# A conv branch's output projection by a seven-product scheme, its outer sums done by accumulating DMAs

## The chip, the cores and the metric

The kernel runs on one core of one Trainium2 chip. The metric is the device time of one execution in microseconds (us). Before the change it is 2522.57 us, the median of three runs (2522.21 to 2522.71).

## The reference

One inference step of a small encoder trunk with two layers. 640 frames (512 of a new stream, 8 x 16 of running streams) of 1024 channels go through, per layer, half a feed-forward step, a mixer, and another half feed-forward step. The change is in the mixer:

```python
z = h @ w_in                       # conv B | conv C | conv V | q | k | v | gates
g = sigmoid(g + b_gate); g_conv, g_attn = split(g)
y_conv = B * causal_conv3(C * V)   # 512 channels
y_attn = band_attention(q, k, v)   # 8 heads of 64
m = g_conv * (y_conv @ w_conv_out) + g_attn * (y_attn @ w_attn_out)
x = x + m @ w_o
```

`w_conv_out` and `w_attn_out` are 512 x 1024, `w_o` is 1024 x 1024, all in fp32.

## The kernel before

Activations lie transposed: channels on the 128 partitions, the 640 frames (T) along the free dimension, in two halves t1 and t2 of 320 columns (HT). A matmul multiplies a 128 x 128 weight tile with 128 x 320 columns. For precision every fp32 operand is split into a high part in fp32r (`hi`, a cast on ScalarE) and a rest (`lo`, a subtraction on VectorE), and a product is three matmuls: hi x hi, lo x hi, hi x lo.

Weights come from one stream in HBM (`wst`), 128 x 1024 at a time, loaded by SyncE's queue (SP) into three buffers `raw`. ScalarE casts each to `whi`, VectorE subtracts to `wlo`; both have three buffers. One such 1024-wide (or 512-wide) weight part is called a slab. `slab()` hands out the next slab and prepares those after it, `flush()` issues VectorE's subtractions that are pending, `quiet()` takes a slab that is ready, `prep` begins one more, `ahead` and `begin` begin the one after.

Many projections are done by a scheme of seven products instead of eight (Strassen's, in Winograd's form), where pairs of row tiles and the two halves of the frames form the 2 x 2 blocks. `gate_pair(m)` (L1263) is one such mixing of two output tiles, m and m + 1, of the gates: seven blocks of twelve matmuls, in the order X11, X21, N6, T5, T7, X22, T4, into three banks pa, pb, pc; four slabs, three of them with sums of weight tiles made on VectorE (four additions of 512 columns). Banks that go on accumulating must be copied out in between: c1 after the first block, u2 after the third, c5 after the fourth (ScalarE); VectorE adds these copies to what comes later, multiplies with rr (the norm's factor), and ScalarE makes the sigmoids.

`outputs` (L1253) is the mixer's last part but for w_o. Its order before: gate pair 2, four products `out(0)` to `out(3)` of w_conv_out, then three times a gate pair and two products (w_conv_out's 4 to 7 behind pairs 4 and 6), then pairs 8 to 14, each with two products of w_attn_out. `product` (L387, matmuls at L374) multiplies all four row tiles of the 512 inputs: 24 matmuls of 320 columns into one two-bank tile py, which VectorE multiplies with the gate. `take`, called in pair 2, splits the four tiles of y_conv. The matmuls of `block` are at L397, the casts of weights at L307, their subtractions at L312, additions at L251.

In this part PE, VectorE and ScalarE run in the order in which the code issues the instructions (`tc.manual_schedule(engines=ORDERED)`); each engine's queue is in order.

`down_rows` (L936) does the feed-forward's second projection by the same scheme and already sends part of its sums by accumulating DMAs from GpSimd's queue (L976).

Of the kernel before, what the change touches and what calls it, by code (L numbers as in the profile page):

```python
# [22 lines left out]
T = SEQ + NB * TS  # L23
HT = T // 2
# [6 lines left out]
KT = D // P  # L31
FT = FF // P
FH = FT // 2
CT = CW // P
# [6 lines left out]
NP = KT // 2  # L41
# [16 lines left out]
XT4, XN6, XT7, X21, X22, X11, XT5 = range(7)  # L58
# [64 lines left out]


def kinds():


    out, inside = [], [False]

    def put(kind):  # L130
        out.append((kind, inside[0]))

    def plain(n):
        for kind in [8] * (n // 8) + [n % 8] * (n % 8 > 0):
# [24 lines left out]
    for l in range(L):  # L159
        ffn(f"a{l}")  # L160
        held = 0
        for what, _ in mixer_order():
            if what == "mix":
# [12 lines left out]


def halves(t):
    return t.rearrange("p (a b) -> p a b", a=2)
# [3 lines left out]
def trunk(ctx: ExitStack, tc: tile.TileContext, xin, wst, small, pbias, samplebias, kcache, vcache,  # L183
# [33 lines left out]
    def tmp(name):  # L217
        return tp.tile([P, UW], F32, tag="t", name=name)[:, :T]
# [31 lines left out]
    def add(out, a, b):  # L250
        DVE.tensor_tensor(out=out, in0=a, in1=b, op=ALU.add)  # L251
# [58 lines left out]
    def flush():  # L310
        for lo, src, hi in pending:
            DVE.tensor_tensor(out=lo, in0=src, in1=hi.bitcast(F32), op=ALU.subtract)  # L312
        pending.clear()
# [73 lines left out]
    def product(ps, ops, at=()):  # L387
        for _ in steps(ps, ops, at):
            pass

    def block(ps, s, half, ops, ks, start, stop):

        for kp in ks:
            w = [z[:, (half * NP + kp) * P : (half * NP + kp + 1) * P] for z in s]
            xh, xl = ops(kp)
            for j, (a, b) in enumerate(((w[0], xh), (w[0], xl), (w[1], xh))):
                PE.matmul(ps, a, b, start=start and kp == 0 and j == 0,  # L397
                          stop=stop and kp == NP - 1 and j == 2, skip_group_check=True)
# [701 lines left out]
    def mixer(l, after):  # L1100
        with tc.tile_pool(name=f"yp{l}", bufs=1, reuse_waits="tile") as yp, \
# [2 lines left out]

            h, st, stats = norm(yp, f"m{l}", O_GM + l * KT, yas[:, 0, :])
            rr = st.rr
            ycp = [yp.tile([P, 2, T], F32, name=f"yc{l}_{c}") for c in range(CT // 2)]
            ycs = [z[:, i] for z in ycp for i in range(2)]
# [78 lines left out]
            with tc.tile_pool(name=f"gp{l}", bufs=1, reuse_waits="tile") as gp, \  # L1187
                 tc.manual_schedule(engines=ORDERED):
                hold[0] = True
                mo = outputs(l, gp, ops.X, st, cs, ycs, yas, sigmoid, gates)  # L1190
        ex = after()
        with tc.manual_schedule(engines=ORDERED):
            hold[0] = True
# [56 lines left out]
        def t5(self, kp):  # L1250
            self.parts(*(z[:, HT:] for z in self.h[2 * kp]), self.a[kp][:, 1])

    def outputs(l, gp, X, st, cs, ycs, yas, sigmoid, gates):  # L1253


        rr, t1, t2 = st.rr, slice(0, HT), slice(HT, T)
        spare = [gp.tile([P, 2, T], F32, name=f"mm{l}_{i}") for i in range(2)]
        mm = ycs + [spare[i // 2][:, i % 2] for i in range(CT)]
        X11, X21, X22, XN6, XT5, XT7, XT4 = (X[i] for i in ("11", "21", "22", "N6", "T5", "T7", "T4"))
        c1, u2, c5 = cs  # L1260
        every = range(NP)

        def gate_pair(m, then=None):  # L1263
            n = f"{l}_{m}"
            pa, pb, pc = (att(f"q{i}{n}")[:, :HT] for i in "abc")
            u, g = gates[m], gates[m + 1] = tmp(f"g{n}"), tmp(f"g{n}_1")
            s0 = quiet()
            block(pa, s0, 0, X11, every, True, True)
            ACT.copy(c1, pa)
            prep(used[0] + 1)  # L1270
            flush()
            if then:
                then()
            block(pb, s0, 1, X21, every, True, True)
            add(u[:, t1], pb, c1)
            s1 = slab(True)[0]
            flush()
            block(pa, s1, 0, XN6, every, False, True)
            ACT.copy(u2, pa)
            block(pc, s1, 1, XT5, every, True, True)  # L1280
            ACT.copy(c5, pc)
            s2 = slab(True)[0]
            block(pa, s2, 0, XT7, every, False, True)
# [4 lines left out]
            block(pc, s2, 1, X22, every, False, True)  # L1288
            add(u[:, t2], pc, u2)
            s3 = slab(True)[0]  # L1290
            DVE.tensor_tensor(out=u, in0=u, in1=rr, op=ALU.mult)
            sigmoid(u, m)
            block(pa, s3, 0, XT4, every, False, True)
            DVE.tensor_tensor(out=g[:, t1], in0=pa, in1=rr[:, t1], op=ALU.mult)
            sigmoid(g, m + 1, -1.0)
            flush()

        def parts(pool, tag, name, src):
# [4 lines left out]
        def out(m, y, then=None):  # L1303

            py = acc(f"py{l}_{m}")
            product(py, y)
            if then:
                then()
            g = gates[m]
            if m < KT:  # L1310
                DVE.tensor_tensor(out=halves(mm[m]), in0=two(py), in1=halves(g), op=ALU.mult)
            else:
                DVE.tensor_tensor(out=halves(g), in0=two(py), in1=halves(g), op=ALU.mult)
                add(mm[m - KT], mm[m - KT], g)
            flush()

        yc, ya, mo = [], [], []

        def take(y, name, srcs):
            for c, src in enumerate(srcs):  # L1320
                y.append(parts(gp, f"y{c}", f"{name}{l}_{c}", src))

        def give(ms):
            for m in ms:
                mo.append(parts(hp, "h", f"m{l}_{m}", mm[m]))

        gate_pair(2, lambda: take(yc, "yc", ycs))
        for m in range(4):
            out(m, yc)
        for m in range(4, 2 * KT, 2):  # L1330
            gate_pair(m, (lambda: take(ya, "ya", [yas[:, c, :] for c in range(CT)])) if m == KT else None)
            y = yc if m < KT else ya
            last = m == 2 * KT - 2
            out(m, y, (lambda: give(range(3))) if last else None)
            out(m + 1, y, (lambda: give(range(3, 6))) if last else None)
        give(range(6, KT))
        return mo

    def attention(l, h, norms, stats, ops, mp, yas, ycp, both, others):
# [421 lines left out]
def _stream(i):  # L1761
# [9 lines left out]
    for l in range(L):  # L1771
# [34 lines left out]
        for what, m in mixer_order():  # L1806
            if what == "v":
                out.append(v.reshape(KT // 2, 2, P, AW).transpose(0, 2, 1, 3).reshape(-1, P, CH))
            elif what == "mix":
                out.append(chunks(held))  # L1810
                held = []

                out.append(chunks([rows[name][a][o::2] for name, a in m for o in range(2)]))
            else:
                held.append(rows[what][m])
        out.append(chunks(held))
# [69 lines left out]
```

## Time and profile before

| | |
|---|---|
| median of 3 runs | 2522.57 us |
| profiled execution | 2522.74 us, span 2521.0 us, granted clock 0.999 |
| TensorE busy | 2502.0 us (99%), 17192 matmuls |
| VectorE busy | 2117.7 us (84%) |
| ScalarE busy | 1325.1 us (53%) |
| GpSimd busy | 185.6 us (7%) |
| DMA | 265.40 MB, mean 105 GB/s |

The profile is of one execution, taken by the hardware profiler. Engines are PE (TensorE matmuls), PEld (its weight loads), DVE (VectorE), ACT (ScalarE), POOL (GpSimd) and SP (SyncE, which issues loads). A row of a timeline gives the start in us, the length, the engine, the line of the kernel, the operation, and the tiles as out<-in; in square brackets stands the idle time just before it and what ended it. A row of groups gives, after the bar, the busy time of the group and the mean of one in ns, and then the idle time before its instructions.

### The profile page before, as it was taken

How to read it: one execution, taken by the hardware profiler on the slowest of the kernel's cores; microseconds unless marked ns; L12 is line 12 of the kernel's file. 1: busy time of each engine (PE TensorE's matmuls, PEld its weight loads, DVE VectorE, ACT ScalarE, POOL GpSimd, SP SyncE). 2: the span in 40 equal slices, each digit the busy share in tenths (PEclk: the TensorE clock that was granted, in tenths of full speed). 3: DMA queues.
4: the chain of work that ended last, by engine and by line, in shares of the span. 5: the costliest groups of instructions: out<-in, count | busy, mean ns of one | idle time of the engine just before them, and what ended most of it. 6: DMA issues, size and time to landing. Idle time of an engine off the chain costs nothing.

```text
span 2521.0 us, 42929 instructions
## 1 busy us (share of the span) xinstructions
PE 2502.0 (99%) x17192; PEld 2441.3 (97%) x17192; DVE 2117.7 (84%) x3347; ACT 1325.1 (53%) x2084; POOL 185.6 (7%) x249
## 2 busy tenths in 40 slices
PE   9999999999999999999999999999999999999998
PEld 9999999888999999999999999998889999999998
DVE  7889888878677899988699999888786768899997
ACT  7445556664444545555455555557644455455553
POOL 0000112111000001000001000021110000010000
PEclk9999999999999999999999999999999999999999
DMA  4233444334222234343224343443342222243434
GB/s 144 76 105 103 115 115 126 107 114 162 76 85 92 75 101 115 105 110 100 84 76 112 110 116 100 115 118 124 129 138 84 76 93 76 86 114 109 123 100 99
DMA packets 99320, 265.40 MB, mean 105 GB/s; under 512 B 9680, under 2 KB 45136, under 8 KB 99120
## 3 DMA queue, kind: packets, MB, share of 16 engines
q1 hardware_dynamic: 69408, 220.76, 26.7%
q0 software_dynamic: 28992, 41.26, 9.3%
q8 instruction: 135, 2.21, 0.4%
q10 hardware_dynamic: 720, 0.65, 0.1%
q14 instruction: 65, 0.53, 0.1%
HBM read 222.70 MB, written 7.94 MB: 91 GB/s over the span
## 4 chain that ended last, share of the span: by engine, by line
PE 92%; ACT 4%; DVE 3%; issue 1%; DMA 0%; DVEq 0%; ACTq 0%
PE pab L397 12%; PE paa L397 11%; PE pcb L397 6%; PE pca L397 6%; PE daa L952 5%; PE py L374 4%; PE po L374 4%; PE qa L397 4%; PE pdb L374 4%; PE dab L952 4%; PE pbb L397 3%; PE pba L397 3%; PE poa L374 2%; PE pda L374 2%; PE pv L1392 2%; PE ma_cv L397 2%
## 5 line engine op out<-in xcount | busy, mean ns | idle before, releaser
L312 DVE TENSOR_TENSOR wlo<-raw,whi 128x1024 fp32r<-128x1024 f32 (+1 forms) x566 | 585.6, 1037 | 177.8 <-ACT whi L307 172.6
L307 ACT CAST whi<-raw 128x1024 fp32r<-128x1024 f32 (+1 forms) x566 | 509.1, 903 | 366.6 <-PE pbb L397 38.6
L307 ACT CAST whi<-s 128x1024 fp32r<-128x1024 f32 (+1 forms) x152 | 144.4, 950 | 279.5 <-issue 89.3
L397 PE MATMUL pab<-xhib,whi 128*128 128x320 f32 x704 | 218.1, 310 | 0.3
L397 PE MATMUL pab<-xhib,wlo 128*128 128x320 f32 x704 | 217.3, 309 | 0.0
L397 PE MATMUL pab<-xlob,whi 128*128 128x320 f32 x704 | 217.2, 309 | 0.0
L397 PE MATMUL paa<-xhia,whi 128*128 128x320 f32 x640 | 198.0, 309 | 1.0 <-ACT c_a L833 0.6
L397 PE MATMUL paa<-xhia,wlo 128*128 128x320 f32 x640 | 197.5, 309 | 0.0
L397 PE MATMUL paa<-xloa,whi 128*128 128x320 f32 x640 | 197.5, 309 | 0.0
L312 DVE TENSOR_TENSOR wlo<-s,whi 128x1024 fp32r<-128x1024 f32 (+1 forms) x152 | 166.3, 1094 | 9.8 <-ACT whi L307 9.8
L397 PEld LDWEIGHTS pab<-xhib,whi 128*128 128x128 f32 x704 | 132.1, 188 | 0.9 <-ACT c_b L833 0.8
L397 PEld LDWEIGHTS pab<-xlob,whi 128*128 128x128 f32 x704 | 132.1, 188 | 0.2
L397 PEld LDWEIGHTS pab<-xhib,wlo 128*128 128x128 f32 x704 | 132.1, 188 | 0.0
L397 PEld LDWEIGHTS paa<-xhia,whi 128*128 128x128 f32 x640 | 120.1, 188 | 1.6 <-ACT c_a L833 0.9
L397 PEld LDWEIGHTS paa<-xloa,whi 128*128 128x128 f32 x640 | 120.1, 188 | 0.1
L397 PEld LDWEIGHTS paa<-xhia,wlo 128*128 128x128 f32 x640 | 120.1, 188 | 0.0
L976 POOL DMA_DIRECT2D x<-c_b x28 | 33.8, 1209 | 1105.6 <-ACT c_b L969 457.8
L397 PE MATMUL pcb<-xhib,wlo 128*128 128x320 f32 x352 | 108.8, 309 | 0.0
L397 PE MATMUL pcb<-xlob,whi 128*128 128x320 f32 x352 | 108.6, 309 | 0.0
L397 PE MATMUL pcb<-xhib,whi 128*128 128x320 f32 x352 | 108.6, 309 | 0.0
L976 POOL DMA_DIRECT2D x<-c_a x36 | 43.6, 1212 | 865.1 <-ACT whi L307 386.4
L251 DVE TENSOR_TENSOR raw<-raw,raw 128x512 f32<-128x512 f32 x152 | 103.7, 683 | 0.8
(681 smaller groups left out, 7943.2 us busy)
## 6 DMA issues: line engine op xcount, KB each, us to landing
raw<-in_wst SPq DMA_DIRECT2D x378, 512.0 KB, 3.5
x<-c_a POOLq DMA_DIRECT2D x36, 320.0 KB, 4.2
x<-c_b POOLq DMA_DIRECT2D x28, 320.0 KB, 4.1
kc<-in_kcache SPq DMA_DIRECT2D x32, 256.0 KB, 3.8
vc<-in_vcache SPq DMA_DIRECT2D x16, 512.0 KB, 4.7
x<-u_a POOLq DMA_DIRECT2D x18, 320.0 KB, 5.4
x<-u_b POOLq DMA_DIRECT2D x14, 320.0 KB, 5.5
bias<-in_pbias POOLq DMA_DIRECT2D x16, 256.0 KB, 3.6
```

The source lines that it names most:

```text
L251: DVE.tensor_tensor(out=out, in0=a, in1=b, op=ALU.add)
L307: ACT.copy(hi[:, d], src[:, c])
L312: DVE.tensor_tensor(out=lo, in0=src, in1=hi.bitcast(F32), op=ALU.subtract)
L374: PE.matmul(ps[:, a, :HT], w, x[:, a * HT : (a + 1) * HT], start=first and j == 0, stop=last and j == 2)
L397: PE.matmul(ps, a, b, start=start and kp == 0 and j == 0, stop=stop and kp == NP - 1 and j == 2, skip_group_check=True)
L952: PE.matmul(ps[u], w, y, start=start and i == 0 and j == 0, stop=i == 1 and j == 2, skip_group_check=True)
L976: POOL.dma_start(rows(r, cols), z, accum_op=ALU.add)
L1392: PE.matmul(pv[t], xx[:, t * P : (t + 1) * P], w[:, kk * AW : (kk + 1) * AW], start=c == 0 and kk == 0 and j == 0, stop=c == KT // 2 - 1 a ...
```

## The change

w_conv_out is no longer computed by eight products but by two calls of a new function `unit`, each for four output tiles: seven blocks of twelve matmuls into two-bank tiles A and B and a pair of banks C. Its operands (`xhi`, `xlo`: X11, X21, X22, T5, T7, T4, N6 for the two pairs of row tiles) are made beforehand in gate pairs 2 and 4 and, for the last `lo` part, in the first unit itself. ScalarE copies the finished sums into the output tile and GpSimd adds the copies made earlier by accumulating DMAs (`put`, `accumulate`). The outputs are kept unweighted and multiplied with the gates later (`weigh`).

The gate pairs 2, 4 and 6 get `direct=False`: VectorE's additions of c1, c5 and u2 are replaced by a ScalarE copy and an accumulating DMA, and the products with rr (`scale`) and the sigmoids (`bend`) are done later, as jobs at named places (`at`, `spot`). In pairs 8 to 14 (`direct=True`) one of three additions is replaced so. The order of the weight stream becomes: gate pairs 2 and 4, unit 0, gate pair 6, unit 4, then pairs 8 to 14 with w_attn_out's products as before.

The core of the diff, cut:

```diff
-    out += gates[:2] + [("co", m) for m in range(4)]
-    for i, g in enumerate(gates[2:]):
-        name, m = ("co", 4 + 2 * i) if i < 2 else ("ao", 2 * i - 4)
-        out += [g, (name, m), (name, m + 1)]
+    out += gates[:3] + [("unit", ("co", 0)), gates[3], ("unit", ("co", 4))]
+    for i, g in enumerate(gates[4:]):
+        out += [g, ("ao", 2 * i), ("ao", 2 * i + 1)]
...
+        def accumulate(out, z):
+            POOL.dma_start(out, z, accum_op=ALU.add)
...
             block(pb, s0, 1, x21, every, True, True)
-            add(u[:, t1], pb, c1)
+            if direct:
+                ACT.copy(u[:, t1], pb)
+                accumulate(u[:, t1], c1)
...
+            if not direct:
+                ACT.copy(u[:, t1], pb)
+                accumulate(u[:, t1], c1)
             block(pa, s2, 0, xT7, every, False, True)
-            add(g[:, t2], pa, c5)
-            DVE.tensor_tensor(out=g[:, t2], in0=g[:, t2], in1=rr[:, t2], op=ALU.mult)
+            if direct:
+                add(g[:, t2], pa, c5)
+            else:
+                ACT.copy(g[:, t2], pa)
+                accumulate(g[:, t2], c5)
...
+        def sum_low(i):
+            return lambda: low(i, slice(0, 4), vs[i])
+        def unit(m0, to):
...
+            s0 = quiet()
+            mul(a, s0, 0, X11, True)
+            copy(z0[:, :, t1], a)
+            prep(used[0] + 1)
+            begin()
+            flush()
+            spot(me, 1)
+            mul(b, s0, 1, X21, True)
+            put(0, t1, b, z0[:, :, t1])
+            s1 = slab(True)[0]
+            flush()
+            mul(a, s1, 0, XN6, False)
+            copy(z0[:, :, t2], a)
+            spot(me, 2)
+            mul(C, s1, 1, XT5, True)
+            copy(z1, C, -1.0)
+            s2 = slab(True)[0]
+            spot(me, 3)
+            mul(a, s2, 0, XT7, False)
+            put(1, t2, a, z1, -1.0)
+            flush()
+            ahead()
+            mul(C, s2, 1, X22, False)
+            put(0, t2, C, z0[:, :, t2])
+            s3 = slab(True)[0]
+            ahead()
+            mul(a, s3, 0, XT4, False)
+            copy(to[:, 1::2, t1], a, -1.0)
+            flush()
+            spot(me, 4)
...
+        at("g2", 1, opening)
+        at("g2", 2, firsts)
+        at("g2", 3, raw_low(0))
+        at("g2", 4, raw_low(1))
+        at("g4", 1, lasts)
+        at("g4", 3, sum_high(0))
+        at("g4", 4, sum_high(1), sum_low(0))
+        at("c0", 1, sum_low(1))
+        at("c0", 2, scale(2))
+        at("c0", 3, bend(2), scale(4))
+        at("c0", 4, bend(4))
+        at("g6", 2, weigh(1, 3))
+        at("g6", 3, weigh(0, 2))
+        at("c4", 2, scale(6))
+        at("c4", 3, bend(6))
+        at("g8", 1, taken(0), taken(1))
+        at("g8", 2, taken(2), weigh(5, 7))
+        at("g8", 3, taken(3))
+        at("g8", 4, weigh(4, 6))
```

`opening` casts X11, X21 and X22 of both pairs on ScalarE (three casts of 640 columns); `firsts` and `lasts` make the sums N6, T5, T7 and T4 on VectorE; `raw_low`, `sum_high` and `sum_low` make the rest of the operands; `taken` splits the four tiles of y_attn.

More of the change, by code (lines that the diff above doesn't have):

```diff
@@ L162, in kinds @@
         for what, _ in mixer_order():
-            if what == "mix":
+            if what in ("mix", "unit"):
                 plain(held)
@@ L1286, in gate_pair @@
+            block(pa, s2, 0, xT7, every, False, True)
+            if direct:
+                add(g[:, t2], pa, c5)
+            else:
+                ACT.copy(g[:, t2], pa)
+                accumulate(g[:, t2], c5)
             flush()
             ahead()
[L1288 to L1293 removed]
+            block(pc, s2, 1, x22, every, False, True)
@@ L1294, in gate_pair @@
+            if direct:
+                add(u[:, t2], pc, u2)
+            else:
+                ACT.copy(u[:, t2], pc)
+                accumulate(u[:, t2], u2)
+            s3 = slab(True)[0]
+            if direct:
+                times(g[:, t2], rr[:, t2])
+                times(u, rr)
+                sigmoid(u, m)
+            block(pa, s3, 0, xT4, every, False, True)
             DVE.tensor_tensor(out=g[:, t1], in0=pa, in1=rr[:, t1], op=ALU.mult)
-            sigmoid(g, m + 1, -1.0)
+            if direct:
+                sigmoid(g, m + 1, -1.0)
@@ L1296, in gate_pair, with scale, job, bend @@
             flush()
+            spot(me, 4)
+        def scale(m):
+            def job():
+                times(gates[m], rr)
+                times(gates[m + 1][:, t2], rr[:, t2])
+            return job
+        def bend(m):
+            def job():
+                sigmoid(gates[m], m)
+                sigmoid(gates[m + 1], m + 1, -1.0)
+            return job
+        v = yc.rearrange("p (i o) (t c) -> p i o t c", o=2, t=2)
+        xhi, xlo = (gp.tile([P, 2, 7, HT], F32R, name=f"x{i}{l}") for i in ("hi", "lo"))
@@ new lines, in outputs, with high, low, opening @@
+        pairs = [{k: (xhi[:, i, c], xlo[:, i, c]) for c, k in enumerate((XT5, XT7, XT4, XN6, X11, X21, X22))}
+                 for i in range(2)]
+        vs = [v[:, i].rearrange("p o t c -> p (o t) c") for i in range(2)]
+        def high(i, c, z):
+            ACT.copy(xhi[:, i, c], z)
+        def low(i, c, z):
+            DVE.tensor_tensor(out=xlo[:, i, c], in0=z, in1=xhi[:, i, c].bitcast(F32), op=ALU.subtract)
+        def opening():
+            high(slice(0, 2), 4, v[:, :, 0, 0])
+            for i in range(2):
+                high(i, slice(5, 7), v[:, i, 1])
@@ new lines, in raw_low, with sum_high, mul, copy @@
+        def raw_low(i):
+            return lambda: low(i, slice(5, 7), v[:, i, 1])
+        def sum_high(i):
+            return lambda: high(i, slice(0, 4), vs[i])
+        def sum_low(i):
+            return lambda: low(i, slice(0, 4), vs[i])
+        def unit(m0, to):
+            n = f"{l}_{m0}"
+            A, B = (acc(f"{i}co{n}") for i in "ab")
+            C = [att(f"c{i}co{n}")[:, :HT] for i in range(2)]
+            a, b = ([z[:, i, :HT] for i in range(2)] for z in (A, B))
+            me = f"c{m0}"
+            def mul(ps, s, half, kind, start):
+                for i in range(2):
+                    for k, pair in enumerate(pairs):
+                        kp = half * NP + 2 * i + k
+                        wh, wl = (z[:, kp * P : (kp + 1) * P] for z in s)
+                        xh, xl = pair[kind]
+                        for j, (w, y) in enumerate(((wh, xh), (wh, xl), (wl, xh))):
+                            PE.matmul(ps[i], w, y, start=start and k == 0 and j == 0,
+                                      stop=k == 1 and j == 2, skip_group_check=True)
+            def copy(out, ps, scale=1.0):
+                for d, z in ((out, two(A if ps is a else B)),) if ps is not C else zip((out[:, 0], out[:, 1]), C):
+                    ACT.activation(d, z, AF.Copy, scale=scale)
+            def put(r, c, ps, z, scale=1.0):
+                copy(to[:, r::2, c], ps, scale)
+                accumulate(to[:, r::2, c], z)
+            s0 = quiet()
[4 more added lines that the diff above has]
+            flush()
+            spot(me, 1)
+            mul(b, s0, 1, X21, True)
[4 more added lines that the diff above has]
+            copy(z0[:, :, t2], a)
+            spot(me, 2)
+            mul(C, s1, 1, XT5, True)
+            copy(z1, C, -1.0)
+            s2 = slab(True)[0]
+            spot(me, 3)
+            mul(a, s2, 0, XT7, False)
[9 more added lines that the diff above has]
+            flush()
+            spot(me, 4)
@@ L1298, in parts, with weigh, job @@
+        def weigh(*ms):
+            def job():
+                for m in ms:
+                    times(mm[m], gates[m])
+            return job
         def parts(pool, tag, name, src):
@@ L1301, in parts, with out @@
             return hi, lo
-        def out(m, y, then=None):
+        ya, mo = [], []
+        def out(m, then=None):
             py = acc(f"py{l}_{m}")
-            product(py, y)
+            product(py, ya)
             if then:
                 then()
[L1309 to L1314, printed above, removed]
+            g = gates[m + KT]
+            DVE.tensor_tensor(out=halves(g), in0=two(py), in1=halves(g), op=ALU.mult)
+            add(mm[m], mm[m], g)
             flush()
[L1317 to L1321, printed above, removed]
         def give(ms):
@@ L1325, in give, with taken, job @@
                 mo.append(parts(hp, "h", f"m{l}_{m}", mm[m]))
[L1327 to L1335, printed above, removed]
+        def taken(c):
+            def job():
+                hi, lo = (z[:, c // 2, :].rearrange("p a b -> p (a b)")[:, (c % 2) * T : (c % 2 + 1) * T]
+                          for z in (xhi, xlo))
+                split(hi, lo, yas[:, c, :])
+                ya.append((hi, lo))
+            return job
+        at("g2", 1, opening)
[17 more added lines that the diff above has]
+        at("g8", 4, weigh(4, 6))
+        gate_pair(2, False)
+        gate_pair(4, False)
+        unit(0, yc)
+        gate_pair(6, False)
+        unit(4, spare)
+        for m in range(0, KT, 2):
+            gate_pair(m + KT, True)
+            last = m == KT - 2
+            out(m, (lambda: give(range(3))) if last else None)
+            out(m + 1, (lambda: give(range(3, 6))) if last else None)
         give(range(6, KT))
+        assert not jobs
         return mo
@@ L1813, in _stream @@
                 out.append(chunks([rows[name][a][o::2] for name, a in m for o in range(2)]))
+            elif what == "unit":
+                out.append(chunks(held))
+                held = []
+                name, a = m
+                out.append(chunks([rows[name][a + r + 2 * u][o::2] for r in range(2) for o in range(2)
+                                   for u in range(2)]))
             else:
```

54 lines of the change are left out of this document (37 added, 17 removed).

## The prediction

> **What bounds the kernel now.** I read the page first (busy times, chain of waits), then the windows of the mixer's output part, where all of the change lies, and then TensorE's, VectorE's and ScalarE's timelines there.
>
> ```profile
> span 2521.0 us, 42929 instructions
> PE 2502.0 (99%) x17192; PEld 2441.3 (97%) x17192; DVE 2117.7 (84%) x3347; ACT 1325.1 (53%) x2084; POOL 185.6 (7%) x249
> ...
> PE 92%; ACT 4%; DVE 3%; issue 1%; DMA 0%; DVEq 0%; ACTq 0%
> ```
>
> TensorE (PE) is the bound: busy for 99% of the span, 92% of the chain. So a matmul that goes is worth its pace, and a wait on TensorE costs its full length; work on other engines costs nothing until TensorE waits for it. The windows of layer 0's output part (gate pair 2, four products, then pairs 4, 6 and 8, each with two products) show how near that is:
>
> ```profile
> 643.80:656.80 13.00, 12.62 (x86) 12.36 (x85) 10.46 (x17) 9.84 (x15) 0.00 (x0) 1.00 0.27 84
> 656.80:670.90 14.10, 14.10 (x98) 14.10 (x97) 8.52 (x12) 3.64 (x5) 0.00 (x0) 1.00 0.22 74
> 670.90:690.30 19.40, 19.40 (x134) 19.40 (x133) 12.54 (x18) 7.54 (x11) 0.00 (x0) 1.00 0.25 82
> 690.30:709.70 19.40, 19.40 (x135) 19.40 (x134) 12.54 (x18) 7.54 (x11) 0.00 (x0) 1.00 0.26 82
> 709.70:729.10 19.40, 19.40 (x134) 19.40 (x134) 16.31 (x23) 9.86 (x15) 0.00 (x0) 1.00 0.26 82
> ```
>
> The columns are length, then busy time of PE, weight loads, VectorE (DVE), ScalarE (ACT) and GpSimd. PE is full except for 0.38 us in the first window; VectorE is busy 60 of 85 us, ScalarE 38. The clock is 1.00 throughout.
>
> **The change, part by part. 1: matmuls that go.** A block is twelve matmuls of 320 columns, and one block follows the other after 674.44 - 672.68 = 1.76 us:
>
> ```profile
> 672.68 0.31 PE L397 MATMUL qb<-hhim,whi 128*128 128x320 f32 x1
> 674.44 0.32 PE L397 MATMUL qa<-thi,whi 128*128 128x320 f32 x1
> ```
>
> So a matmul costs 1.76 / 12 = 0.1467 us of PE (the 0.31 of its row overlaps with the next). w_conv_out now takes 8 products x 4 row tiles x 3 terms x 2 halves = 192 matmuls a layer; the two units take 2 x 7 blocks x 12 = 168. 24 less a layer, 48 in all: -7.04 us. The Trainium skill (TensorE: Matmul & The Clock Gate, Back-to-back issue gap) gives an isolated warm matmul a gap of columns / 2.4 + 2.5 ns, which for 320 columns is an estimated 136 ns and would make the saving 6.5 us; the trace's own pace decides, so 7.04 stands.
>
> **2: a stall that goes.** In gate pair 2, ScalarE casts four operands (yc) between the first copy and the copy that frees bank pa for its next accumulation:
>
> ```profile
> 647.00 1.05 ACT L307 CAST whi<-raw 128x1024 fp32r<-128x1024 f32 x1
> 647.94 0.73 ACT L221 CAST yc_0hi<-yc 128x640 fp32r<-128x640 f32 x1
> 648.57 0.73 ACT L221 CAST yc_1hi<-yc 128x640 fp32r<-128x640 f32 x1
> ...
> 650.45 0.62 ACT L307 CAST whi<-raw 128x512 fp32r<-128x512 f32 x1
> 650.97 0.42 ACT L1279 COPY capsm<-qa 128x320 f32<-128x320 f32 x1
> 651.29 0.43 ACT L1281 COPY c<-qc 128x320 f32<-128x320 f32 x1
> ```
> ```profile
> 650.47 0.31 PE L397 MATMUL qc<-hhim,whi 128*128 128x320 f32 x1
> 651.45 0.41 PE L397 MATMUL qa<-thi,whi 128*128 128x320 f32 x1 [0.38 <-ACT capsm L1279]
> ```
>
> The last three matmuls of block 4 begin at 650.47, so block 5 was due at 650.91 and began at 651.45: 0.54 us lost. `opening` puts three casts there, not four; one is worth 648.57 - 647.94 = 0.63 us, so the copy ends at 650.76, in time. Layer 1 shows the same wait: -1.08 us.
>
> **3: VectorE's queue into the first unit.** The built kernel's order there (it follows from `spot(me, 1)` standing behind `flush()` in `unit`): gate 4's last product with rr; the two halves of wlo of weight slab 1; operand lows of pair 0 (`sum_low(0)`, 1280 columns); one addition of weights; wlo of slab 2, which needs ScalarE's cast of that sum; wlo of slab 3; only then `sum_low(1)`, without which block 3 (N6) can't take its second row pair, from its fifth matmul on. The prices are start-to-start steps of these rows:
>
> ```profile
> 649.22 0.82 DVE L222 TENSOR_TENSOR yc_0lo<-yc,yc_0hi 128x640 fp32r<-128x640 f32 x1
> 649.96 0.82 DVE L222 TENSOR_TENSOR yc_1lo<-yc,yc_1hi 128x640 fp32r<-128x640 f32 x1
> ...
> 652.17 0.48 DVE L251 TENSOR_TENSOR g<-qb,capsm 128x320 f32<-128x320 f32 x1
> 652.57 0.68 DVE L312 TENSOR_TENSOR wlo<-raw,whi 128x512 fp32r<-128x512 f32 x1
> ...
> 654.51 1.22 DVE L312 TENSOR_TENSOR wlo<-raw,whi 128x1024 fp32r<-128x1024 f32 x1
> 655.65 0.48 DVE L251 TENSOR_TENSOR g<-qc,capsm 128x320 f32<-128x320 f32 x1
> ...
> 668.34 0.68 DVE L312 TENSOR_TENSOR wlo<-s,whi 128x512 fp32r<-128x512 f32 x1
> 668.94 0.69 DVE L312 TENSOR_TENSOR wlo<-raw,whi 128x512 fp32r<-128x512 f32 x1
> ```
> ```profile
> L557 DVE TENSOR_TENSOR xlob<-xob,xhib 128x960 fp32r<-128x960 f32 x8 | 9.2, 1153 | 0.7 <-ACT xhib L542 0.7
> ```
> ```profile
> 676.21 0.31 PE L397 MATMUL qc<-hhim,whi 128*128 128x320 f32 x1
> ```
> ```profile
> 676.41 0.42 ACT L1279 COPY capsm<-qa 128x320 f32<-128x320 f32 x1 [1.24 <-PE qa L397]
> ```
>
> 320 columns step 0.40, 512 step 0.60, 640 step 0.74, 1024 step 1.14. 640 columns last 0.82 and 960 last 1.153, so 1280 last about 1.49 (step 1.41): an estimate from these two. A result is free to read 676.41 - 676.21 = 0.20 us after PE's next block begins. From the unit's start U: gate 4's last block can be read at U + 0.20; then 0.40 + 2 x 0.60 + 1.41 + 0.68 (a sum of 512, to its end) = U + 3.89; ScalarE's cast 1.05 and two handovers of 0.03 = U + 5.00; wlo 1.14 + 0.60, then `sum_low(1)` 1.49 and 0.06 to PE = U + 8.29. PE stands before its fifth matmul of block 3 at U + 2 x 1.76 + 4 x 0.147 = 4.11. The wait is about 4.2 us a layer, and hangs on no backlog from before: it begins with PE's own last block. Bounds: 3.8 if each step is 5% shorter, 4.8 if the cast comes half a us later. For two layers: +8.4.
>
> **4: ScalarE's queue in both units.** After block 4 it copies bank C (two of 320 columns), casts the next slab (1024), does two sigmoids (`bend`), and only then copies bank a, which block 7 needs.
>
> ```profile
> L966 ACT ACTIVATE c_a<-daa 128x640 f32<-128x640 f32 x18 | 12.7, 705 | 3.5 <-PE daa L952 1.6
> L969 ACT ACTIVATE c_a<-dca 128x320 f32<-128x320 f32 x36 | 15.6, 434 | 2.8 <-PE dca L952 2.5
> L1117 ACT ACTIVATE g<-g,sm 128x640 f32<-128x640 f32 x32 | 25.1, 825 | 11.9 <-DVE g L1291 11.9
> ```
>
> Steps: 2 x 0.33 (434 ns less the overlap of 0.1 that 650.97 and 651.29 show), 0.94 (647.00 to 647.94), 2 x 0.73 (825 ns with the same overlap), then 0.705, with 0.20 before and 0.06 after: 4.03 us from block 4's end, where PE needs it after two blocks, 3.52. 0.5 a unit (0 to 1), four units: +2.1.
>
> **5: the rest, costed at nothing.** Accumulating DMAs take the additions of pairs 2, 4 and 6, and of half of each later pair, off VectorE; ScalarE pays a copy of 0.43. Each issue holds POOL's queue, which is empty there (0.00 in the windows).
>
> ```profile
> x<-c_a POOLq DMA_DIRECT2D x36, 320.0 KB, 4.2
> ```
> ```profile
> DMA to landing us min/median/max: 4.1/4.7/7.4
> ```
>
> A transfer of 160 KB isn't in the trace; 4.2 is taken, with 7.4 as the far end. Its readers come later: in pairs 8 to 14 `times(u, rr)` waits for a DMA issued 4.2 us into the pair (two blocks, 0.20, the copy 0.43) and runs after block 6, at about 11.6; 4.2 + 7.4 = 11.6 is just in time. Queued behind it on VectorE are the next pair's weights. The three weight slabs more a layer and their sums lie on VectorE and ScalarE between the waits above; they are fullest in pair 8. From 3.4 us into it (block 1, 0.20, ScalarE's copy 0.33 and cast 1.05) VectorE has 1.14 + 0.60 of weights, four ya lows and two `weigh` products (6 x 0.74), some 0.4 of waiting for the last ya cast (the pair's own copies stand ahead of it), 0.40, and 1.22 for the next product's weights: ready at 11.6, where PE takes them at 7 x 1.76 + 2 x 0.147 = 12.6. If this cover of 1.0 us goes, I put 1 to 2 us a layer on it. SP issues as many weight loads as before.
>
> **Sum.** -7.04 - 1.08 + 8.4 + 2.1 = +2.4 us on the profiled execution's 2522.74 (span 2521.0): 2525.1; the median of the runs shown, 2522.57, lies 0.17 lower, so I say 2525.0. With the bounds of the waits (3.8 and no ScalarE wait; 4.8 and 1.0 in each unit) this case runs from 2522 to 2528.
>
> **The rivals.** *The unit doesn't wait on `sum_low(1)`*, because VectorE has room on average (60 of 85 us busy). Then 2522.6 - 7.0 - 1.1 + 2.1 = 2516.6, and 2514.5 without ScalarE's waits as well. Against it: the queue runs in order and the seven steps begin at a result of PE. Chance 0.20.
>
> *The clock drops after the wait*; it ends on the other side. PE has no gap of 4 us between matmuls in this trace, but its first ones, after 5.86 us of waiting, are slow:
>
> ```profile
> 5.86 0.90 PE L374 MATMUL poa<-hhia,whi 128*128 128x320 f32 x2 [5.86 <-ACT whi L620]
> ...
> 10.38 0.74 PE L374 MATMUL poa<-hhia,wlo 128*128 128x320 f32 x2
> 10.91 0.72 PE L374 MATMUL poa<-hhia,whi 128*128 128x320 f32 x2
> ...
> 12.07 0.45 PE L374 MATMUL poa<-hhia,whi 128*128 128x320 f32 x2
> 12.36 0.46 PE L374 MATMUL poa<-hloa,whi 128*128 128x320 f32 x2
> ```
>
> A pair steps 0.53 us until 11.2 and 0.29 after: 5.3 us at little over half pace, a loss of 5.3 x (1 - 0.29/0.53) = 2.4 us. If a wait of 4.2 us is enough, it is paid once a layer: 2527.4 if one layer has it, 2529.8 if both do, slower by 0.29%. The point from which it decides lies somewhere below 5.86 us. The Trainium skill (TensorE: Matmul & The Clock Gate, HAM oscillation) puts it at gaps of over about 3.4 us; by that rule the wait of part 3 is past it, and no run here shows such a gap in the middle of work. Chance 0.15, since the gap must also fall well for whatever watches it.
>
> *VectorE falls behind in pair 8* and its cover of 1.0 us goes: 2527 to 2529. Chance 0.13. That the change doesn't do what it says is out: the built kernel has 168 matmuls in the two units.
>
> **How the numbers follow.** 0.52 for the sum, 0.20, 0.15 and 0.13 for the rivals. A measurement of this kernel can tell about 0.2%, 5 us, from no change. Faster: the first rival, 0.20. Slower: half or more of the clock and VectorE cases and the upper end of the sum, where waits add up, 0.30. Same: 0.50. The range takes in the first rival at 2516.6 and both clock drops: 2516 to 2530; the sum's own range is 2522 to 2528.
>
> **What would show it.** In each layer PE should wait once for VectorE's xlo for about 4.2 us within the first unit, and four times in all about 0.5 us for ScalarE's copy of bank a; pair 2's wait for the copy should be gone; 48 matmuls fewer; the clock 1.00 after the wait, or the windows below 1.00 if the second rival is right. I am wrong if PE flows through the first unit, or if it waits in pair 8 and after.

## The result and the profile after

| | before | after |
|---|---|---|
| median, 11 runs each | 2522.61 us (2522.00 to 2524.04) | 2528.77 us (2527.35 to 2529.49) |
| profiled execution, its span | 2522.74 us, 2521.0 us | 2527.53 us, 2525.8 us |
| granted clock | 0.999 | 0.996 |
| TensorE | 2502.0 us, 17192 matmuls | 2499.1 us, 17144 matmuls |

The changed kernel is slower: ratio 1.0024, 95% interval 1.0016 to 1.0031, or 6.2 us. The prediction said 2525.0 us, in a range of 2516 to 2530, with "the same" as the likeliest of the three. The time lies in the range, but 3.8 us above the number and above the sum's own range of 2522 to 2528; what lifts it is the second rival. By the prediction's own mark of about 5 us this is "slower", which had 0.30. The page of the changed kernel:

```profile
PE 2499.1 (99%) x17144; PEld 2436.8 (96%) x17144; DVE 2132.5 (84%) x3359; ACT 1363.4 (54%) x2160; POOL 222.8 (9%) x287
```

48 matmuls fewer, as forecast, and yet a longer span. The windows of layer 0's output part (the first unit, then the end of the second and pair 8), and as the last row the first unit of layer 1; columns as in the prediction, the granted clock third from the end:

```profile
668.50:685.00 16.50, 12.42 (x69) 12.16 (x68) 10.62 (x14) 8.32 (x13) 1.82 (x2) 0.79 0.47 107
...
710.00:730.00 20.00, 20.00 (x136) 19.66 (x135) 17.33 (x26) 12.13 (x21) 3.34 (x3) 1.00 0.62 140
1915.30:1932.00 16.70, 12.59 (x75) 12.32 (x74) 11.95 (x16) 8.41 (x15) 3.83 (x4) 0.90 0.59 143
```

Apart from short waits of 0.24 us, one in each unit, TensorE loses time in one place of each layer, the first unit: 4.08 us idle there in layer 0, and in the same window a clock of 0.79. TensorE's timeline around the wait:

```profile
672.27 0.31 PE L1400 MATMUL aco<-xhi,whi 128*128 128x320 f32 x1
676.65 0.63 PE L1400 MATMUL aco<-xlo,whi 128*128 128x320 f32 x1 [4.08 <-DVE xlo L1360]
677.09 0.47 PE L1400 MATMUL aco<-xhi,wlo 128*128 128x320 f32 x1
677.35 0.47 PE L1400 MATMUL aco<-xhi,whi 128*128 128x320 f32 x1
...
681.62 0.34 PE L1400 MATMUL c1co<-xlo,whi 128*128 128x320 f32 x1
```

The fifth matmul of block 3 should have followed 672.27 by 0.147 us; it begins 4.38 us later, so the wait costs 4.23 us. Then the step from one matmul to the next is 0.266 us instead of 0.147, for 17 matmuls, until 681.62: 17 x 0.12 = 2.04 us more. Layer 1 has the same: a wait of 4.27 us, then 13 slow matmuls, 1.51 us:

```profile
1922.46 0.31 PE L1400 MATMUL aco<-xhi,whi 128*128 128x320 f32 x1
1926.88 0.41 PE L1400 MATMUL aco<-xlo,whi 128*128 128x320 f32 x1 [4.11 <-DVE xlo L1360]
...
1927.59 0.47 PE L1400 MATMUL aco<-xhi,wlo 128*128 128x320 f32 x1
```

Here the first matmuls after the wait still run at the full pace of 0.15; the slow ones begin 0.7 us after the restart. The granted clock says when it fell. Two windows for each layer, cut where the clock changes:

```profile
671.43:674.84 3.41, 1.15 (x8) 0.88 (x7) 2.24 (x4) 1.56 (x2) 0.00 (x0) 1.00 0.00 0
674.85:681.66 6.81, 5.00 (x19) 5.01 (x20) 4.03 (x6) 1.84 (x3) 1.20 (x1) 0.50 0.74 202
...
1924.12:1927.53 3.41, 0.65 (x4) 0.65 (x5) 3.41 (x5) 0.59 (x1) 0.00 (x0) 1.00 0.49 163
1927.54:1930.94 3.40, 3.40 (x15) 3.40 (x14) 1.56 (x4) 1.24 (x3) 1.20 (x1) 0.50 0.75 202
```

In layer 0 the clock is at a half from 674.84 on, while TensorE still waits, for 6.83 us; in layer 1 from 1927.54 on, for 3.41 us. The slow matmuls are those in these two stretches.

The account of the two spans: matmuls -7.04; pair 2's wait -1.28 (0.54 and a restart of 0.10, twice); the two waits +8.50 and their restarts +0.20 (any matmul after a wait is followed after 0.25, not 0.147); the slow matmuls +3.74 (2.04, 1.51, and 0.19 more at layer 0's restart); ScalarE's waits in the units +0.96 (below). That makes +5.1, against the +4.8 that the spans differ by.

### The profile page after: what moved, and what is told of

It reads as the page before. It is cut to its first block, busy times and chain, and to the rows that moved or that the text cites. A ratio compares the mean times of both kernels' runs of the same rounds, so it can differ in the third digit from the quotient of the medians.

```text
span 2525.8 us, 43051 instructions
## 1 busy us (share of the span) xinstructions
PE 2499.1 (99%) x17144; PEld 2436.8 (96%) x17144; DVE 2132.5 (84%) x3359; ACT 1363.4 (54%) x2160; POOL 222.8 (9%) x287
## 5 line engine op out<-in xcount | busy, mean ns | idle before, releaser
L250 DVE TENSOR_TENSOR raw<-s,raw 128x512 f32<-128x512 f32 x156 | 107.4, 688 | 0.0
```

## The experiments

All are edits of the changed kernel, but the seventh. Medians are of 8 to 10 runs, next to before on the same chip (2522.41 us in the first four, 2522.69 in the next four, 2522.47 in the last). My theory after the result: the wait for `sum_low(1)` and the drop of the clock that it sets off make up the loss. The rival to that: the slow matmuls are of something else that lies there (DMA traffic, a weight load in the way), and would stay without a wait.

**1. TensorE kept busy in the wait.** 28 matmuls into a bank that nobody reads, ahead of block 3; nothing else is altered, so VectorE's queue is as late as before.

```diff
+            if m0 == 0:
+                idle = att(f"idle{n}")[:, :HT]
...
+            if m0 == 0:
+                for _ in range(28):
+                    PE.matmul(idle, s1[0][:, :P], pairs[0][X11][0], start=True, stop=True)
             mul(a, s1, 0, XN6, False)
```

> The changed kernel, and in the first unit of each layer 28 matmuls of 320 columns into a bank that nobody reads, just ahead of block N6, so that TensorE works through most of the 4.2 us in which it waited for sum_low(1). Theory (wait plus clock: the clock drops because TensorE stands still): the wait shrinks to about 0.1 us behind 4.1 us of idle work, the granted clock stays at 1.00 in the unit, and the time falls by the 3.9 us that the slow matmuls cost (0.117 us each, about 19 in layer 0 and 13 in layer 1), from 2528.8 to about 2525. Rival (the slow matmuls have another cause, such as the unit's own operands or the transfers beside it): they stay slow and the time stays at 2528 to 2529.

Measured: 2524.08 us (2523.70 to 2524.78), ratio 1.0007, interval 0.9998 to 1.0016. The windows over the first unit of each layer, then TensorE's timeline at the 28:

```profile
666.00:690.00 24.00, 24.00 (x162) 23.50 (x161) 17.29 (x24) 16.99 (x28) 6.28 (x6) 1.00 0.61 128
1913.00:1936.00 23.00, 23.00 (x155) 22.50 (x154) 17.47 (x24) 16.10 (x26) 6.29 (x6) 1.00 0.55 121
```
```profile
672.26 4.27 PE L1426 MATMUL idle<-xhi,whi 128*128 128x320 f32 x28
676.37 0.31 PE L1402 MATMUL aco<-xhi,whi 128*128 128x320 f32 x1
```

The needless work takes as long as the wait did (4.11 us to the next matmul), a rest of 0.13 us of waiting stays, and the clock is 1.00 with no slow matmul. So it is TensorE's standing still that brings the low clock, not what else runs there: 28 x 2 matmuls of pure waste make the kernel 4.7 us faster. By the profiled run the drops were worth 3.7; the median of the changed kernel's runs lies 1.2 above its profiled run.

**2. `sum_low(1)` made in pair 4.**

```diff
-        at("g4", 4, sum_high(1), sum_low(0))
-        at("c0", 1, sum_low(1))
+        at("g4", 4, sum_high(1), sum_low(0), sum_low(1))
```

> The changed kernel with sum_low(1) issued at the end of gate pair 4, ahead of the first unit's weight slabs in VectorE's queue. Theory: the chain to it loses the addition, the cast and two wlo (0.68 + 1.11 + 1.14 + 0.60 = 3.5 us), so the wait falls from 4.2 to about 0.7 us a layer, no clock drop follows, and the time falls by 2 x 3.5 + 3.9 = 10.9 us to about 2518. Rival (VectorE is short of time as a whole, so the wait turns up elsewhere, at the slab that now comes later): 2522 or more, with a new wait for wlo in block T7.

Measured: 2517.53 us (2517.11 to 2518.10), ratio 0.9980, interval 0.9971 to 0.9990. In VectorE's queue the operand stands ahead of the addition and the two subtractions now, and so doesn't wait for ScalarE's cast either; what is left of the wait is 0.63 us, with a short one for ScalarE's copy two blocks later:

```profile
673.23 0.41 PE L1400 MATMUL aco<-xlo,whi 128*128 128x320 f32 x1 [0.48 <-DVE xlo L1360]
676.69 0.41 PE L1400 MATMUL aco<-xhi,whi 128*128 128x320 f32 x1 [0.25 <-ACT z L1405]
```

No slow matmul follows. One job moved in a queue takes 11.2 us off the changed kernel: 7.2 of waiting and 3.7 of drops, 0.8 given back in short waits, and the 1.2 by which the changed kernel's median lies above its profiled run.

**3. The sigmoids behind the copy of bank a.**

```diff
             s2 = slab(True)[0]
-            spot(me, 3)
             mul(a, s2, 0, XT7, False)
             put(1, t2, a, z1, -1.0)
+            spot(me, 3)
```

> The changed kernel with the jobs of a unit's third place (two sigmoids on ScalarE, in the first unit scale(4) on VectorE too) issued after the copy of bank a instead of before it. Theory: the four waits of 0.24 us before the units' last blocks go, 1.0 us in all, and the large wait and the clock drop stay: about 2527.8. Rival (the copy waits for something else than the sigmoids): the four waits stay and so does the time, 2528.8.

Measured: 2526.99 us (2525.55 to 2529.49), ratio 1.0018, interval 1.0009 to 1.0027. The waits before the units' last blocks are gone, the two of VectorE are as they were (4.08 idle in both layers), and slow matmuls follow them again, 9 and 13 of them. The median falls by 1.8 where the four waits had cost 0.96; the rest lies within the spread of these runs, 3.9 us. One source of such a spread is the clock: in layer 0 of the profiled run it is at a half for 3.41 us, in the changed kernel's for 6.83.

**4. Both, and pair 4's jobs ahead of its last instructions.** As 2 and 3, but with the three jobs set between the steps of `gate_pair` that follow its sixth block.

```diff
+            spot(me, 5)
             s3 = slab(True)[0]
...
+            spot(me, 6)
             DVE.tensor_tensor(out=g[:, t1], in0=pa, in1=rr[:, t1], op=ALU.mult)
...
+            spot(me, 7)
             flush()
...
+        at("g4", 5, sum_high(1))
+        at("g4", 6, sum_low(0))
+        at("g4", 7, sum_low(1))
```

> e3, and gate pair 4 reordered: sum_high(1) ahead of the weight casts of the first unit's slab 1 on ScalarE, sum_low(0) and sum_low(1) around gate 4's last product on VectorE, ahead of wlo of slab 1. Theory (the seven-product scheme saves 7.0 us of TensorE and pair 2's wait 1.2 us; all that was lost came from VectorE's and ScalarE's order and the clock that followed): no wait of TensorE over 0.3 us in the units, clock 1.00, 2522.6 - 8.2 + 0.4 = about 2514.8. Rival (VectorE's added work is the bound): waits of 1 us or more elsewhere, 2518 to 2522.

Measured: 2516.28 us (2515.42 to 2517.36), ratio 0.9976, interval 0.9966 to 0.9985. The waits for VectorE are gone; what keeps it from the forecast is one short wait a layer, 0.57 us and a restart, before block 5 (T7):

```profile
676.22 0.42 PE L1403 MATMUL aco<-xhi,whi 128*128 128x320 f32 x1 [0.42 <-ACT z L1408]
```

**5 and 6. Waits of a middle length.** As 2, with `sum_low(1)` made twice (5) or three times (6), each one more of 1280 columns on VectorE. The question was from which length a wait lowers the clock.

```diff
+        at("g4", 4, sum_high(1), sum_low(0), sum_low(1), sum_low(1))
```

> e2 with sum_low(1) done twice (the second writes the same values), so that its end comes 1.41 us later. Theory (a wait costs its length, and the clock drops only behind a wait long enough): the wait in the first unit is 0.64 + 1.41 = 2.05 us a layer. If 2 us is below the point, no matmul is slow and the time is 2517.5 + 2.8 = 2520.3; if any wait of this kind drops the clock, 2 to 4 us more, 2522 to 2524.

> e2 with sum_low(1) done three times: a wait of 0.64 + 2 x 1.41 = 3.46 us a layer, 0.8 less than in the changed kernel. Without a drop 2517.5 + 5.6 = 2523.1. If the point from which the clock drops lies near the page's 3.4 us and hangs on how the wait falls in a window that runs by itself, some runs drop and some don't: runs spread over 2523 to 2525. If it lies well below 3.4, as much as in the changed kernel is lost, 3.9 us: 2527.

Measured: 2521.98 us (2520.72 to 2522.97) with two, 2525.92 us (2525.47 to 2527.27) with three; ratios 0.9996 (0.9987 to 1.0005) and 1.0013 (1.0004 to 1.0022). The last section explains why the windows are cut as they are, 3.41 us each. With two, the wait in layer 0 lies in one of them, that in layer 1 in two:

```profile
672.93:676.34 3.41, 1.55 (x11) 1.28 (x9) 3.38 (x3) 0.00 (x0) 0.00 (x0) 1.00 0.01 1
...
1918.80:1922.21 3.41, 2.17 (x13) 1.64 (x12) 3.38 (x4) 0.82 (x2) 0.00 (x0) 1.00 0.14 21
1922.21:1925.62 3.41, 2.43 (x16) 2.44 (x17) 2.23 (x3) 1.80 (x3) 0.00 (x0) 1.00 0.00 0
```

With three, the wait in layer 1 lies in two windows, and in the third the clock is at a half (in layer 0 from 677.54 to 680.95):

```profile
1920.00:1923.41 3.41, 1.72 (x12) 1.47 (x10) 3.38 (x3) 0.12 (x1) 0.00 (x0) 1.00 0.07 9
1923.41:1926.82 3.41, 1.55 (x10) 1.56 (x11) 2.37 (x3) 0.92 (x1) 0.00 (x0) 1.00 0.00 0
1926.82:1930.23 3.41, 3.41 (x15) 3.41 (x14) 3.25 (x5) 2.64 (x7) 1.20 (x1) 0.50 0.26 70
```

After waits of 2.17 and 2.38 us the clock stays at 1.00; after 3.70 us, in both layers, 13 matmuls are slow (1.5 us each time). From 2 to 6 the medians rise by 8.4 us: the waits by 6.1, two drops of 1.5, and the waits for ScalarE, 0.4 in each layer, that the longer wait swallows: 8.3. From 2 to 5 they rise by 4.45, the waits by 3.3. That 1.2 more isn't explained. The profiled run of 5 came to the part 1.5 us later than that of 6, and lost that at the kernel's very start. Other runs of 5 may have had a drop, which isn't shown: the mean granted clock of one (2522.94 us) is 0.997, as in the profiled runs with drops; that of five is 0.999, and their median, 2521.01, lies 3.5 above experiment 2.

**7. Pair 2's wait, in the kernel before.** The casts of the operands are put behind the copy that frees bank pa (in pair 8 too, which has its own casts there and had no such wait); all else is the kernel before.

```diff
             block(pa, s1, 0, xN6, every, False, True)
-            if then:
-                then()
...
             ACT.copy(u2, pa)
+            if then:
+                then()
```

> The kernel before with the four casts of yc in gate pair 2 issued after the copy of N6's bank instead of before X21. Theory (step 2 of the prediction): the wait before block T7 of pair 2 goes, 0.54 and 0.1 of restart a layer: 2522.4 - 1.2 = 2521.2. Rival (the copy waits for something other than the casts, or the casts only move the wait to the copy of block T5's bank): 2522.4.

Measured: 2521.63 us (2521.18 to 2522.22), ratio 0.9996, interval 0.9986 to 1.0005; the median is 1.06 us lower and the span 1.6, and no wait over 0.13 us is left in pair 2 of either layer. The interval holds 1, so the time alone doesn't settle it; the trace does.

**8. Pairs 2 and 4 without the separate steps.** The fourth experiment's kernel with `direct=True` for pairs 2 and 4, without the jobs that `scale` and `bend` do for them. It asks what the separate products and sigmoids are worth.

```diff
-        at("c0", 2, scale(2))
-        at("c0", 3, bend(2), scale(4))
-        at("c0", 4, bend(4))
...
-        gate_pair(2, False)
-        gate_pair(4, False)
+        gate_pair(2, True)
+        gate_pair(4, True)
```

> e4 with gate pairs 2 and 4 done as pairs 8 to 14 are: two of three sums, the products with rr and the sigmoids in the pair itself, so that the operand casts of the first unit compete with them. Theory (VectorE's queue in pair 4 is what decides the first unit's wait): VectorE gets 0.40 + 0.40 + 0.40 + 0.74 = 1.9 us more ahead of sum_low in pair 4, and the first unit waits about 2 us a layer: 2516.3 + 4 = about 2520. Rival (the accumulating DMAs and the later scaling are not needed, VectorE has room): 2516.3.

Measured: 2526.79 us (2525.38 to 2527.75), ratio 1.0015, interval 1.0005 to 1.0025: 10.5 us above the fourth, far more than expected. ScalarE's, VectorE's and TensorE's timelines at the place:

```profile
674.10 0.83 ACT L1117 ACTIVATE g_4b<-g_4b,sm 128x640 f32<-128x640 f32 x1 [0.97 <-DVE g_4b L1334]
674.84 0.68 ACT L1408 ACTIVATE z<-aco 128x640 f32<-128x640 f32 x1
```
```profile
672.18 1.48 DVE L1363 TENSOR_TENSOR xlo<-yc,xhi 128x1280 fp32r<-128x1280 f32 x1
673.59 0.48 DVE L1334 TENSOR_TENSOR g_4b<-qa,rrm 128x320 f32<-128x320 f32 x1
```
```profile
675.57 0.42 PE L1403 MATMUL aco<-xhi,whi 128*128 128x320 f32 x1 [2.30 <-ACT z L1408]
```

The windows of the wait and of what follows it:

```profile
673.41:676.82 3.41, 1.25 (x7) 1.00 (x8) 3.41 (x6) 1.42 (x2) 0.00 (x0) 1.00 0.00 0
676.82:680.23 3.41, 3.41 (x15) 3.41 (x14) 2.24 (x3) 2.77 (x4) 0.18 (x1) 0.50 0.00 0
```

A sigmoid stands in ScalarE's queue ahead of the copy that frees bank a, and waits for a product that stands in VectorE's queue behind `sum_low(0)`. So the unit's third block waits, 2.46 us in layer 0 and 3.27 in layer 1, and both waits are followed by 13 slow matmuls. These two make 5.7 us; the waits in pairs 2 and 4 (0.24 and 0.84 in layer 0, 0.23 and 0.81 in layer 1) 2.1, six restarts 0.6, the two drops 3.25, less the fourth's own waits of 1.35: 10.3 of the 10.5 us. Sigmoids in place would do better with `sum_low(0)` elsewhere, which wasn't run; what is shown is that the separate steps uncouple ScalarE's queue from VectorE's, and that a coupling here costs this much.

**9. The fourth, with its last wait removed.** In the fourth, ScalarE's copy for `put(0, t1, b, ...)` came ahead of the copy of bank a.

```diff
             mul(b, s0, 1, X21, True)
-            put(0, t1, b, z0[:, :, t1])
...
             copy(z0[:, :, t2], a)
+            put(0, t1, b, z0[:, :, t1])
```

> The fourth experiment's kernel with one move more: ScalarE's bend of the low half's tail is put behind its copy of bank a in the unit. If the 0.57 us wait before block T7 of the first unit is ScalarE's queue (the copy of z behind the bend), it goes in both layers, with the 0.10 us after it: 2516.28 - 2 * 0.6 = about 2515.1. If something else holds block T7 there (the bank's earlier reader, say), the wait stays and the time is 2516.3. Rival: the moved bend comes late for VectorE's sum and delays the second unit: 2517 or more.

The expectation speaks of a sigmoid (`bend`); what the edit moves is the copy out of bank b, which stood in the same place of the queue. Measured: 2515.35 us (2514.66 to 2516.09), ratio 0.9972, interval 0.9962 to 0.9983. The copy of bank a comes first in ScalarE's queue and the wait before block 5 is gone from both layers, but half of it comes back: TensorE, 0.57 us earlier now, stands 0.29 us before the third block of pair 6, since the copy of its bank is queued behind pair 4's two sigmoids. ScalarE's timeline at both places, and TensorE's at the second:

```profile
674.74 0.70 ACT L1408 ACTIVATE z<-aco 128x640 f32<-128x640 f32 x1
675.33 0.70 ACT L1408 ACTIVATE yc<-bco 128x640 f32<-128x640 f32 x1
...
683.51 0.82 ACT L1117 ACTIVATE g_4b<-g_4b,sm 128x640 f32<-128x640 f32 x1
684.23 0.41 ACT L1292 COPY z<-qa 128x320 f32<-128x320 f32 x1
```
```profile
684.25 0.31 PE L396 MATMUL qb<-hhim,wlo 128*128 128x320 f32 x1
684.69 0.42 PE L396 MATMUL qa<-thi,whi 128*128 128x320 f32 x1
```

This is the best version: 7.1 us faster than the kernel before, 13.4 faster than the changed one. Its span of 2513.4 us is 7.6 below that of before: 8.3 for the matmuls and pair 2's wait, less 0.8 for this new one.

## Why the prediction came out as it did

**Step 1 (48 matmuls, 7.04 us) held.** The page shows 17144, and experiment 9, where new waits cost 0.8 us in all and pair 2's wait is gone too, comes out 7.1 us below the kernel before.

**Step 2 (pair 2's wait) held.** ScalarE's queue in pair 2 after the change, three casts in one row, then (behind a cast of weights) the copy, and TensorE's next block:

```profile
647.69 1.98 ACT L1357 CAST xhi<-yc 128x640 fp32r<-128x640 f32 x3
...
650.10 0.42 ACT L1303 COPY capsm<-qa 128x320 f32<-128x320 f32 x1
```
```profile
650.66 0.33 PE L396 MATMUL qa<-thi,whi 128*128 128x320 f32 x1
```

The copy ends 0.14 us before TensorE needs the bank. The wait was worth a little more than 0.54, since its restart of 0.10 goes too. Experiment 7 takes the same wait out of the kernel before by another way.

**Step 3 (VectorE's queue, 4.2 us a layer) held to the tenth.** The walk can be set beside VectorE's timeline; the unit begins at 668.31:

```profile
668.51 0.49 DVE L1332 TENSOR_TENSOR g_4b<-qa,rrm 128x320 f32<-128x320 f32 x1 [0.48 <-PE qa L396]
...
670.12 1.49 DVE L1360 TENSOR_TENSOR xlo<-yc,xhi 128x1280 fp32r<-128x1280 f32 x1
671.52 0.69 DVE L250 TENSOR_TENSOR raw<-s,raw 128x512 f32<-128x512 f32 x1
673.37 1.83 DVE L311 TENSOR_TENSOR wlo<-raw,whi 128x1024 fp32r<-128x1024 f32 x2 [1.17 <-ACT whi L306]
675.11 1.49 DVE L1360 TENSOR_TENSOR xlo<-yc,xhi 128x1280 fp32r<-128x1280 f32 x1
```

The first product begins 0.20 after TensorE's block, the sum ends at 672.21 (forecast 668.31 + 3.89 = 672.20), VectorE stands 1.17 us for ScalarE's cast, and TensorE goes on at 676.65 (forecast 668.31 + 8.29 = 676.60). The 1.49 us put on an operand of 1280 columns, which the trace of before didn't have, was right. Experiment 2 moves that one job, and the wait shrinks to 0.63.

**Step 4 (ScalarE's queue, 0.5 us in each of four units) was mis-sized: 0.24.** ScalarE's timeline after block 4 of the first unit, and TensorE's at block 7:

```profile
680.79 0.44 ACT L1405 ACTIVATE capsm<-c0co 128x320 f32<-128x320 f32 x1 [0.90 <-PE c0co L1400]
682.14 0.44 ACT L1405 ACTIVATE capsm<-c1co 128x320 f32<-128x320 f32 x1 [0.92 <-PE c1co L1400]
682.48 1.04 ACT L306 CAST whi<-raw 128x1024 fp32r<-128x1024 f32 x1
683.42 1.55 ACT L1117 ACTIVATE g<-g,sm 128x640 f32<-128x640 f32 x2
684.87 0.69 ACT L1405 ACTIVATE yc<-aco 128x640 f32<-128x640 f32 x1
```
```profile
685.32 0.31 PE L1400 MATMUL c1co<-xhi,wlo 128*128 128x320 f32 x1
685.61 0.41 PE L1400 MATMUL aco<-xhi,whi 128*128 128x320 f32 x1
```

The order was right, but I had both copies of bank C run after block 4. The first of them, c0's, is free to run once its six matmuls are done, in the block's second half. One copy's 0.33 less, the path is 3.70 instead of 4.03, against 3.52 that the cover lasts; measured, 685.61 - 681.95 = 3.66. The wait is 0.14 and the restart 0.10, so 0.96 for four units and not 2.1.

**Step 5 (nothing) held.** The accumulating DMAs of 160 KB land after 3.4 to 4.2 us (4.2 had been taken), those of 320 KB after 4.2 to 6.6 (medians by tile), and TensorE waits for none:

```profile
g<-capsm POOLq DMA_DIRECT2D x12, 160.0 KB, 4.0
...
mm<-z POOLq DMA_DIRECT2D x4, 320.0 KB, 6.6
```

In pair 8 the next product's weights were due 11.6 us into the pair with 1.0 us of cover. The pair begins at 712.39, and the subtraction, last of the queue I had written down, runs to 724.02, 11.63 us in, so this rival's condition wasn't met:

```profile
722.80 1.22 DVE L311 TENSOR_TENSOR wlo<-raw,whi 128x1024 fp32r<-128x1024 f32 x1
```

**The clock rival was the one that came, and the step that failed is its chance.** I gave it 0.15, on the ground that the gap "must also fall well for whatever watches it". That ground holds for waits of about 2.4 us (2.38 without a drop in experiment 5, 2.46 with one in 8), but not for these: in the profiles here every wait of 3.27 us or longer in the middle of work was followed by slow matmuls, seven out of seven (two each in the changed kernel, in 3 and in 6, one in 8), one of them a wait of 3.70 cut nearly in halves. The rule of the Trainium skill (TensorE: Matmul & The Clock Gate, HAM oscillation), gaps of over about 3.4 us, named the waits of 4.2 rightly and deserved more weight. It isn't the bound in this kernel to the tenth, though: waits of 2.46 and 3.27 us dropped the clock too. The price of 2.4 us a drop, taken from the kernel's start, was near: 2.2 and 1.5, with the clock at a half for 6.8 and 3.4 us, of which 1.8 in layer 0 were waiting anyway.

So with the steps as measured but without the drops, 2522.74 - 7.04 - 1.28 + 8.70 + 0.96 = 2524.1. Experiment 1, which has no drop, measured 2524.08, 1.7 above the kernel before on its chip where this sum has 1.3; that the two agree to the hundredth is luck. The number 2525.0 was near for a TensorE whose clock doesn't react, by a sum in which one term was 1.1 too large; the clock put 3.7 on top in the profiled run, and 4.7 lie between the medians of the changed kernel and of experiment 1.

## What to carry to other kernels

Where the bounding engine has nothing to do for some microseconds, the price is more than the wait: count the slow instructions after it too, and if the wait can't be removed, see whether it can be shortened to about two microseconds (2.38 us was the longest here without a drop, 2.46 the shortest with one) or filled with work that nobody needs. A change that removes work from the bound is lost at once if one operand is made behind an unrelated chain in an in-order queue; walk that queue from the last result it depends on, instruction by instruction, and ask for each whether the waited-for job could stand ahead of it. Where two banks are filled one after the other, the copy of the first can begin while the second is being filled.

## What the runs showed of the hardware

The granted clock changes only on a grid of 3.41 us that runs by itself. In the changed kernel it falls at 674.84, comes back at 681.67, falls at 1927.54 and comes back at 1930.95 us: 2, 365 and 1 steps of 3.413 us apart. In every profile these changes lie whole steps behind the clock's first rise, which comes 8.9 to 14.2 us after the span's start, so the grid lies differently in each run. (In 5, where no drop shows the edges, the windows are counted from its first rise at 14.16.)

The clock is at a half for one step after seven of the eight waits that drop it, and for two in the changed kernel's layer 0, where 1.8 us of the first of the two were still part of the wait. It may fall while TensorE waits (674.84, with the restart at 676.65) or up to 1.25 us after (experiment 8: 676.82, with the restart at 675.57). A matmul of 320 columns then steps 0.266 us instead of 0.147. So 9 to 17 matmuls are slow, and a drop costs 1.1 to 2.2 us, by where the wait falls on the grid.

The length of the wait alone doesn't decide, as 2.38 us without a drop and 2.46 with one already suggest; it is how long TensorE stands still within one step. The idle time in a step is the window's length less TensorE's busy time. In the eight drops, in the step just before, it is 1.86 us (experiment 6, layer 1: 3.41 - 1.55) to 3.41 (experiment 3, layer 0). In the steps of this part without a drop after them it is 1.86 at most (experiment 5, layer 0); the wait of 2.38 us, in layer 1 of 5, is cut by an edge into 1.24 and 0.98, while 2.16 of the 2.46 us of experiment 8 lie in one step. So the bound here is near 1.9 us of 3.41, to a few hundredths that these rows leave open. It is worked out from steps full of 320-column matmuls; at the kernel's end, with smaller ones, the clock also fell after steps with less idle time (0.69 us in experiment 2), so it isn't a bound for all work.

The medians spread for more reasons than this. The changed kernel's runs lie within 2.1 us and experiment 3's within 3.9, but the kernel before, without any drop in its profile, has one set of 12 runs within 0.7 and one of 11 within 2.0.
